# HGRN scores of a hybrid decoder trunk: two heads at a time with the levels sent one by one, against four heads at a time with the levels copied and sent as one block

## The chip, the cores and the metric

The kernel runs on one core of a Trainium2 chip, in one launch. The core has five engines with an instruction queue each: TensorE (PE; matrix products, with the loads of its stationary operand shown as PEld), VectorE (DVE), ScalarE (ACT), GpSimd (POOL) and SyncE (SP), which here only issues transfers. The metric is the device time of one execution in microseconds. Before the change it was 1250.81 us, the median of 3 runs (1249.93 to 1252.86). A chance given below is for a time that is faster or slower by more than 0.2%.

## The reference, cut to what matters

The model is a trunk of four layers on 256 tokens of width 1024. Layers 0 and 3 mix tokens with HGRN2, layer 1 with an mLSTM, layer 2 with S5; each is followed by a SwiGLU block of 2816 hidden columns. Only HGRN2 is touched here:

```python
q, f, v, g = jnp.split(x @ w_in, 4, axis=-1)
log_f = jnp.logaddexp(jnp.log(lb), jnp.log1p(-lb) + jax.nn.log_sigmoid(f))
k = (1.0 - lb) * jax.nn.sigmoid(-f)
q = jax.nn.silu(q)
...
    b = jnp.cumsum(lfb, axis=2)
    decay = jnp.exp(jnp.where(mask[:, :, None], b[t] - b[s], -jnp.inf))
    att = jnp.einsum('bhtd,bhsd,bhtsd->bhts', qb, kb, decay)
    o = att @ v + (q * exp(b)) @ s_prev
...
o = _head_rmsnorm(o, norm_w) * jax.nn.silu(g)
return o @ w_out
```

There are 8 heads with 128 key channels each. The score of query token t and key token s is a sum over the channels of q[t] k[s] times the product of the forget gates of all tokens from s+1 to t. The lower bound lb is zero in layer 0 and is not in layer 3.

## The kernel before

All weights come from HBM in float32, in blocks of 128 x 2048 (1 MB). `stage_next` (L113) splits each block for the products: ScalarE casts a half of 1024 columns to its high part (`hi`, L150), VectorE takes the difference as its low part (`lo`, L151), and `mm3` (L178) does a product as three, high by high, low by high and high by low (L181 to L183). Four blocks of such halves can be held; a block is staged one block ahead of its use (`AHEAD`), and the transfers are issued by SyncE in the order of the list that `plan` (L1362) writes. A projection with the weights as the stationary operand (`ws_block`, L198; two heads per block, 48 products of 256 columns) gives gates and queries with channels on the partitions; `as_part` (L185) gives values and output gates with tokens on the partitions, in products of 512 columns. `pieces` (L510) cuts such a projection into four pieces of 12 products that can be placed between other work.

The HGRN stage (`hgrn`, L485) runs in this order: values of the first half of the heads, the gates of all four head pairs (`hgrn_gates`, L606; five steps on ScalarE and two on VectorE for a pair, and four more on ScalarE where there is a lower bound), a change of ScalarE's table set, the queries of two pairs, and then the scores. `hgrn_scores` (L626) is a generator for one pair of heads. The tokens of the two halves of the sequence lie in one tile; the second half is reversed, so that both halves share each operation. The scores within blocks of tokens are built in levels m = 1, 2, 4, ... 64. At level m the keys of one block of m tokens meet the queries of the next block. Before a level, keys and queries have been multiplied up with the gate products that reach to the border between the two blocks; after it, they are multiplied on (`mul(x, x, whose(e, m, y))`, L683) and the gate products are paired (L687). This is the walk.

What goes to TensorE in a pair: 16 narrow products for the diagonal (L650), 8 for each of m = 1 to 16 (L664), 8 for m = 32 and 8 for m = 64 (L673), all with a stationary operand of 32 columns, each into one quarter of the partitions; and 2 full products for the scores across the two halves (L696). For m below 32 ScalarE first copies the keys of the level into `kk` (L660), and VectorE writes the results into the 32 x 32 blocks of the tile `near` with `copy_predicated` under a mask (L667). At m = 32 VectorE copies `near` into the score tile (L676), and ScalarE copies the levels 32 and 64 there (L680). Each level ends with a `yield`.

`scores` (L575) advances the generators of two pairs in turn, one level each, and puts other work between the levels:

```python
scores((0, 1), ([], [lambda: query(2)], [], [lambda: query(3)], v1[0:1], v1[1:2], v1[2:3], v1[3:]))
scores((2, 3), ([lambda: late.append(heads_out(0))], g0[0:1], ...
```

`heads_out` (L534) multiplies the scores of four heads with the values (L544, L546), squares and sums for the norm of the heads; `turn` (L560) gates the result and transposes it (`head_turn`, L448, L452); `out_proj` (L427) is the output projection with the two layer norms.

The framework's planner orders each engine's instructions: it takes the ready instruction of the highest priority (the order in the program) by a cost model, and sets all semaphores. `order` (L140) and the table dependencies in `act` and `table` (L82 to L99) are edges that only fix an order in this plan. Tiles with the same tag share a set of buffers; the banks of PSUM come in tags "a" (4), "g" (2) and "t" (2).

Of the kernel before, what the change touches and what calls it, by code (L numbers as in the profile page):

```python
# [28 lines left out]
MASKED = (1, 2, 4, 8, 16)  # L29
BIG = 1e30  # L30
# [4 lines left out]
class Trunk:  # L35
# [449 lines left out]
    def hgrn(self, j, gb, lb=None):  # L485
# [3 lines left out]
        with tc.tile_pool(name=self.uid("hg"), bufs=1, reuse_waits="tile") as hp, \  # L489
                tc.tile_pool(name=self.uid("hw"), bufs=2, reuse_waits="tile") as wp:  # L490
            msk = hp.tile([P, len(MASKED) + 1, 64], F32, name=self.uid("msk"))
            atts = [hp.tile([P, 512], F32, name=self.uid("att")) for _ in range(3)]
            for t in atts:
                nc.gpsimd.memset(t, 0.0)
            ot = self.transposed(hp)
# [38 lines left out]
            def heads_out(n):  # L534

                ss = self.small.tile([P, 2, 4], F32, tag="ss", name=self.uid("ss"))
                po = [self.bank("a") for _ in range(2)]
                for h in range(2):
                    for e in range(4):
                        hd = 4 * n + e  # L540
                        att, cross = mem[hd // 2]
                        c = slice(hd * P, (hd + 1) * P)
                        o = po[h][:, e * P : (e + 1) * P]
                        nc.tensor.matmul(o, att[:, 2 * h + hd % 2, :], v[:, h, c], start=True, stop=h == 0)  # L544
                        if h:
                            nc.tensor.matmul(o, cross[:, hd % 2, :], v[:, 0, c], start=False, stop=True)  # L546
# [5 lines left out]
                def scaled():  # L552
                    for h in range(2):
                        on[n, h] = wp.tile([P, 512], F32, tag="q", name=self.uid("on"), bufs=4)
                        f4 = lambda x: x.rearrange("p (a b) -> p a b", a=4)
                        nc.vector.tensor_tensor(f4(on[n, h]), f4(po[h]), r[:, 4 * h : 4 * h + 4, None].broadcast_to([P, 4, P]), ALU.mult)
# [8 lines left out]
            mem, q, pre, on = {}, {}, {}, {}  # L565

            def query(pr):
                pq = pair_proj(4 + pr, "a")
                q[pr] = wp.tile([P, 512], F32, tag="q", name=self.uid("q"), bufs=4)
                self.act(q[pr], pq, AF.Silu)  # L570

            def gates(pr):
                pre[pr] = self.hgrn_gates(wp, pr, pair_proj(8 + pr), lb)

            def scores(prs, fill):  # L575

                runs = [self.hgrn_scores(wp, q[pr], *pre[pr], msk, atts[pr % 3]) for pr in prs]
                for todo in fill:
                    for pr, run in zip(prs, runs):
                        mem[pr] = next(run)  # L580
                    for f in todo:
                        f()
# [3 lines left out]
            self.table("natural_log_exp_and_others")  # L586
# [19 lines left out]
    def hgrn_gates(self, wp, pr, pf, lb):  # L606

        nc, act = self.nc, self.act
        k, f = (wp.tile([P, 512], F32, tag=t, name=self.uid(t), bufs=4) for t in "kf")
# [3 lines left out]
        act(l, l, AF.Ln, bias=1.0)  # L613
        nc.vector.scalar_tensor_tensor(f, pf, 0.0, l, ALU.min, ALU.subtract)
# [3 lines left out]
        if lb is not None:  # L618
            for i in range(2):
                hd = slice(2 * pr + i, 2 * pr + i + 1)  # L620
                x, y = (t.rearrange("p (h a t) -> p a h t", h=2, a=2)[:, i] for t in (f, k))
                act(x, x, AF.Identity, scale=lb[:, 1, hd], bias=lb[:, 0, hd])
                act(y, y, AF.Copy, scale=lb[:, 1, hd])
        return k, f

    def hgrn_scores(self, wp, q, k, f, msk, att):  # L626

# [11 lines left out]
        keys = lambda t, m: view(t, 0, (256 + m, 2), (2 * m, P // m), (1, m))  # L639
        queries = lambda t, m: view(t, m, (256 - m, 2), (2 * m, P // m), (1, m))  # L640
        whose = lambda e, m, s: view(e, s, (2 * P // m + 1 - 2 * s, 2), (2, P // m), (0, m))
        four = lambda x: x.rearrange("p (a t) -> p a t", a=4)
        heads = lambda x: x.rearrange("p (a t) -> p a t", a=2)
        rows = lambda c: slice(32 * c, 32 * c + 32)
        near = wp.tile([P, P], F32, tag="near", name=self.uid("near"))
        k4, q4, a4 = four(k), four(q), four(att)
        pd = self.bank("a")[:, 0:P]
        for i in range(4):
            for c in range(4):
                nc.tensor.matmul(pd[rows(c), rows(i)], k4[:, i, rows(c)], q4[:, i, rows(c)], start=True, stop=True)  # L650
        nc.vector.tensor_tensor(four(near), four(pd), msk[:, len(MASKED), None, 0:32].broadcast_to([P, 4, 32]), ALU.mult)
        mul(q, q, f)
        e, ends = f, wp.tile([P, 256], F32, tag="ends", name=self.uid("ends"))
        spare = 0
        for m in (1, 2, 4, 8, 16, 32, 64):
            n = P // (2 * m)
            pl = self.bank("a")
            if m < 32:
                kk = wp.tile([P, 2 * P], F32, tag="kk", name=self.uid("kk"))
                nc.scalar.copy(view(kk, 0, (m, 2), (2 * m, 2 * n), (1, m)), keys(k, m))  # L660
                pl = pl[:, 0:64]
                for i in range(2):
                    for c in range(4):
# [854 lines left out]
```

## Time and profile before

| What | Value |
| --- | --- |
| median of 3 runs | 1250.81 us (1249.93 to 1252.86) |
| the profiled execution's own time | 1250.21 us |
| span of the profile | 1248.4 us |
| TensorE, VectorE, ScalarE busy | 1228.9, 957.0, 694.1 us |
| granted TensorE clock | 0.998 |
| in 13 to 130 us (layer 0's HGRN): TensorE, VectorE, ScalarE | 116.84, 92.48, 73.43 us |
| in 920 to 1046 us (layer 3's HGRN): the same | 125.13, 97.21, 79.25 us |

The span runs from the first to the last instruction. In rows of the order of time the columns are start, length, engine, line, operation, output and inputs, shape, count; equal instructions that follow each other are merged into one row. A product of two float32 tiles shows as two records, a product of the split parts as one. In rows of groups the numbers behind the bar are the busy time, the mean length of one in ns, and the idle time before them with what ended it. The end of a matmul is modelled, so the distance between starts says more than the length.

### The profile page before, as it was taken

To read this page: it belongs to the slowest core of one execution; us is meant where nothing else is said; L and a number is where in the kernel's file an instruction comes from. 1 tells how busy PE (TensorE), PEld (TensorE's weight loads), DVE (VectorE), ACT (ScalarE), POOL (GpSimd) and SP (SyncE) were. 2 spreads that over 40 slices of the span, in tenths; PEclk is the share of its full clock that TensorE was granted. 3 is DMA by queue.
4 is the path that set the end of the run, shared out by engine and by line. 5 is a ranking of instruction groups with operands and counts; after the bars stand their busy time and mean duration, and the time that the engine had idled before them with its cause. 6 is when DMAs were issued, how large, how long until landed. Compare 5 with 4: busy or idle time off the path is not lost.

```text
span 1248.4 us, 21395 instructions
## 1 busy us (share of the span) xinstructions
PE 1228.9 (98%) x8464; PEld 1030.2 (83%) x8464; DVE 957.0 (77%) x1717; ACT 694.1 (56%) x1126; POOL 34.7 (3%) x60
## 2 busy tenths in 40 slices
PE   9999999999999999999998999999999999999997
PEld 7978888888798888888886788888889878888886
DVE  6887879797787799887599787666486887766664
ACT  6755575565467555555444355555359653555551
POOL 0000100000100100000000000000000000000000
PEclk9999999999999999999999999999999999999999
DMA  8833376666273278767656456555446432755530
GB/s 313 303 136 136 142 276 221 214 223 236 97 301 135 102 277 300 240 249 249 219 203 222 169 191 248 189 182 202 169 180 216 155 133 104 268 186 185 195 143 34
DMA packets 50244, 247.91 MB, mean 199 GB/s; under 512 B 6336, under 2 KB 15952, under 8 KB 23776
## 3 DMA queue, kind: packets, MB, share of 16 engines
q1 hardware_dynamic: 50016, 246.46, 54.9%
q8 instruction: 66, 1.08, 0.3%
q14 instruction: 34, 0.28, 0.1%
q0 software_dynamic: 128, 0.09, 0.0%
HBM read 233.94 MB, written 12.58 MB: 197 GB/s over the span
## 4 chain that ended last, share of the span: by engine, by line
PE 89%; DVE 5%; DMA 2%; ACT 2%; issue 1%; SPq 0%; DVEq 0%; POOL 0%; ACTq 0%
PE g L211 18%; PE g L181 10%; PE g L183 10%; PE g L182 10%; PE g L214 9%; PE a L182 8%; PE a L181 8%; PE a L183 8%; DVE lo L151 1%; PE a L370 1%; PE t L272 1%; DMA bc<-in_s_bc 1%; PE a L664 1%; DMA first<-in_first 1%; PE a L544 1%; DVE s5rot L1218 1%
## 5 line engine op out<-in xcount | busy, mean ns | idle before, releaser
L151 DVE TENSOR_TENSOR lo<-w,hi 128x1024 fp32r<-128x1024 f32 x388 | 470.9, 1222 | 117.2 <-ACT hi L150 109.8
L150 ACT CAST hi<-w 128x1024 fp32r<-128x1024 f32 x388 | 405.1, 1051 | 186.7 <-PE a L182 95.6
L211 PE MATMUL g<-xx,hi 128*128 128x512 f32 x1024 | 356.4, 397 | 0.4 <-DVE sum L352 0.3
L214 PE MATMUL g<-xx,lo 128*128 128x256 f32 x1024 | 264.9, 279 | 0.0
L211 PEld LDWEIGHTS g<-xx,hi 128*128 128x128 f32 x1024 | 186.0, 188 | 37.1 <-DVE sum L352 1.1
L214 PEld LDWEIGHTS g<-xx,lo 128*128 128x128 f32 x1024 | 193.2, 189 | 10.9
L181 PE MATMUL g<-hi,xx 128*128 128x512 f32 (+1 forms) x416 | 166.3, 401 | 3.0 <-ACT xx L291 2.0
L183 PE MATMUL g<-lo,xx 128*128 128x512 f32 (+1 forms) x416 | 164.0, 396 | 0.1
L182 PE MATMUL g<-hi,xx 128*128 128x512 f32 (+1 forms) x416 | 163.2, 393 | 0.0
L182 PE MATMUL a<-hi,hl 128*128 128x512 f32 x328 | 129.5, 395 | 0.0
L183 PE MATMUL a<-lo,hh 128*128 128x512 f32 x328 | 129.4, 395 | 0.0
L181 PE MATMUL a<-hi,hh 128*128 128x512 f32 x328 | 129.0, 394 | 0.0
L351 ACT COPY sum<-g 128x256 f32<-128x256 f32 x128 | 47.7, 372 | 142.3 <-PE g L211 142.1
L352 DVE TENSOR_TENSOR sum<-g,sum 128x256 f32<-128x256 f32 x128 | 54.1, 423 | 61.8 <-ACT sum L351 61.3
L181 PEld LDWEIGHTS g<-hi,xx 128*128 128x128 f32 x416 | 78.2, 188 | 20.0 <-ACT xx L291 3.5
L183 PEld LDWEIGHTS g<-lo,xx 128*128 128x128 f32 x416 | 78.1, 188 | 17.5 <-DVE lo L151 1.9
L182 PEld LDWEIGHTS g<-hi,xx 128*128 128x128 f32 x416 | 78.3, 188 | 14.6
L182 PEld LDWEIGHTS a<-hi,hl 128*128 128x128 f32 x328 | 61.6, 188 | 14.6 <-DVE hl L341 0.5
L183 PEld LDWEIGHTS a<-lo,hh 128*128 128x128 f32 x328 | 61.7, 188 | 13.5
L181 PEld LDWEIGHTS a<-hi,hh 128*128 128x128 f32 x328 | 61.6, 188 | 13.1 <-ACT hh L340 0.5
L181 PE MATMUL g<-xx,hi 128*128 128x256 f32 x192 | 54.5, 284 | 0.0
L183 PE MATMUL g<-xx,hi 128*128 128x256 f32 x192 | 54.5, 284 | 0.0
(307 smaller groups left out, 1733.7 us busy)
## 6 DMA issues: line engine op xcount, KB each, us to landing
w<-in_w_gu SPq DMA_DIRECT2D x88, 1024.0 KB
w<-in_w_dn SPq DMA_DIRECT2D x44, 1024.0 KB
w<-in_w_hg SPq DMA_DIRECT2D x30, 1024.0 KB
w<-in_w_ml SPq DMA_DIRECT2D x12, 1024.0 KB
gb<-in_ln SPq DMA_DIRECT2D x8, 1024.0 KB
w<-in_w_ho SPq DMA_DIRECT2D x8, 1024.0 KB
w<-in_w_so SPq DMA_DIRECT2D x8, 1024.0 KB
w<-in_w_mo SPq DMA_DIRECT2D x4, 1024.0 KB
```

The costliest lines, as they stand in the source:

```text
L150: self.nc.scalar.copy(hi, x)
L151: i = self.nc.vector.tensor_tensor(lo, x, hi.bitcast(F32), ALU.subtract).ins
L181: mm(ps, lh, rh, start=start, stop=False)
L182: mm(ps, ll, rh, start=False, stop=False)
L183: mm(ps, lh, rl, start=False, stop=stop)
L211: whole = lambda: mm(ps, hi[:, c], self.xx[:, k].rearrange("p i t -> p (i t)"), start=k == 0, stop=k == KD - 1)
L214: mm(ps[:, S:], lo[:, c], self.xh[:, k], start=False, stop=False)
L272: nc.tensor.transpose(pt[:, (k % 4) * P : (k % 4 + 1) * P], z[:, k * P : (k + 1) * P], self.ident)
L351: nc.scalar.copy(t, ps[:, S:])
L352: nc.vector.tensor_tensor(t, ps[:, 0:S], t, ALU.add)
L370: nc.tensor.matmul(down[h][n], hidden(h, j, b)[x], dn[j][b][y][:, f], start=False, stop=(x, y, b) == steps[-1])
L544: nc.tensor.matmul(o, att[:, 2 * h + hd % 2, :], v[:, h, c], start=True, stop=h == 0)
```

## The change

`hgrn_scores` now works on four heads (a quad): its tiles of keys, queries and gates have 1024 columns instead of 512, and the multiplications of the walk cover four heads each. The levels m = 1 to 32 no longer go to TensorE as the walk gets to them. For each, ScalarE copies the level's keys and its queries into buffers (`saved`), and the walk goes on. When all six have been multiplied through, one block of instructions sends the level 64 and then the saved levels to TensorE (`tiny`, with an order edge behind the walk's last multiplication), into two PSUM banks. Five masked copies into `near` on VectorE follow, then copies into the score tile on ScalarE, the one of `near` among them. The diagonal products also have an edge that keeps them together.

`hgrn` asks for gates and queries of two pairs, begins the walk of the first quad, and puts the gates and queries of the other two pairs and two pieces of values behind it in the program; the score block of the first quad comes after these. The second quad follows in the same way, with pieces of values and output gates. ScalarE's table set is now changed four times in a stage instead of twice. There is one score tile in place of three; `near`, `ends` and `cross` have one buffer; the tiles of the transposed output are allocated at the end, in the buffers of the saved levels. The masks become wider, and the list of weights follows the new order.

```diff
+NEAR = MASKED + (32,)
...
             def query(pr):
                 pq = pair_proj(4 + pr, "a")
-                q[pr] = wp.tile([P, 512], F32, tag="q", name=self.uid("q"), bufs=4)
-                self.act(q[pr], pq, AF.Silu)
+                self.act(part(pr // 2, "q", pr), pq.rearrange("p (h x) -> p h x", h=2), AF.Silu)
...
-            for pr in range(4):
-                gates(pr)
+            gates(0)
+            gates(1)
             nc.sync.dma_start(msk, self.a["c_lvl"])
             nc.sync.dma_start(nw, self.a["hg_nw"][j])
-            self.table("silu_and_others")
+            self.table(silu)
             query(0)
             query(1)
             v1 = pieces(v, AF.Copy, 0, 1)
             g0, g1 = (pieces(g, AF.Silu, 12, n) for n in range(2))
-            scores((0, 1), ([], [lambda: query(2)], [], [lambda: query(3)], v1[0:1], v1[1:2], v1[2:3], v1[3:]))
-            late = []
-            scores((2, 3), ([lambda: late.append(heads_out(0))], g0[0:1], g0[1:2] + [lambda: late.pop()()], g0[2:3], g0[3:], g1[0:1], g1[1:2], g1[2:3]))
+            first = scores(0)
+            walk(0, first, len(NEAR))
+            self.table(exp)
+            gates(2)
+            gates(3)
+            self.table(silu)
+            query(2)
+            query(3)
+            v1[0]()
+            v1[1]()
+            walk(0, first)
+            second = scores(1)
+            walk(1, second)
+            v1[2]()
+            walk(0, first)
+            walk(1, second, len(NEAR) - 1)
+            v1[3]()
+            g0[0]()
+            g0[1]()
+            late = heads_out(0)
+            g0[2]()
+            late()
+            for f in g0[3:] + g1[:3]:
+                f()
+            walk(1, second)
+            g1[3]()
+            walk(1, second)
             gb = gb()
-            g1[3]()
+            ot = tuple(hp.tile([P, KD, S], F32R, tag="o", name=self.uid(n), bufs=2) for n in ("oh", "ol"))
...
-        for m in (1, 2, 4, 8, 16, 32, 64):
-            n = P // (2 * m)
-            pl = self.bank("a")
-            if m < 32:
-                kk = wp.tile([P, 2 * P], F32, tag="kk", name=self.uid("kk"))
-                nc.scalar.copy(view(kk, 0, (m, 2), (2 * m, 2 * n), (1, m)), keys(k, m))
...
+        for i in (2, 3, 6, 7, 0, 1, 4, 5):
             for c in range(4):
-                nc.tensor.matmul(pd[rows(c), rows(i)], k4[:, i, rows(c)], q4[:, i, rows(c)], start=True, stop=True)
+                mm = nc.tensor.matmul(pd[rows(c), rows(i)], k8[:, i, rows(c)], q8[:, i, rows(c)], start=True, stop=True).ins
+                self.order(mm, lead)
+                lead = lead or mm
...
+        for g, m in enumerate(NEAR):
+            n = 512 // m
+            kc, qc = saved[2 * g : 2 * g + 2]
+            nc.scalar.copy(view(kc, 0, (m, 2), (2 * m, 256 // m), (1, m)), keys(k, m))
+            nc.scalar.copy(view(qc, 0, (256, 2), (m, 256 // m), (1, m)), queries(q, m))
+            for x, y in ((keys(k, m), 1), (queries(q, m), 0)):
+                last = mul(x, x, whose(e, m, y)).ins
+            new = ends[:, 0:n]
+            if m > 1:
+                new, spare = f[:, spare : spare + n], spare + n
+            mul(new, e[:, 0::2], e[:, 1::2])
+            e = new
             yield
+        pl = [self.bank("a") for _ in range(2)]
+
+        def tiny(o, x, y):
+            self.order(nc.tensor.matmul(o, x, y, start=True, stop=True).ins, last)
...
+        level = lambda g: pl[g // 4][:, g % 4 * P : (g % 4 + 1) * P]
+        for g, m in enumerate(NEAR):
+            kc, qc = saved[2 * g : 2 * g + 2]
+            for a in range(4):
+                for c in range(4):
...
+                    tiny(o, kc[:, a * P + 32 * c :][:, 0:32], y)
+        for g, m in enumerate(MASKED):
+            three = lambda x: x.rearrange("p (h b m) -> p h b m", h=2, m=m)
+            nc.vector.copy_predicated(view(near, m, (P - m, 2), (2 * m, 64 // m), (1, m)), three(i32(msk[:, g * P : (g + 1) * P])), three(level(g)))
+        for c in range(4):
+            nc.scalar.copy(a8[rows(c), :, rows(c)], eight(near[rows(c)]))
...
-            p += [("w_hg", j, s) for s in (0, 1, 8, 9, 10, 11, 4, 5, 6, 7, 2, 3, 12, 13, 14, 15)] + [("w_ho", j, s) for s in range(4)]
+            p += [("w_hg", j, s) for s in (0, 1, 8, 9, 4, 5, 10, 11, 6, 7, 2, 3, 12, 13, 14, 15)] + [("w_ho", j, s) for s in range(4)]
```

More of the change, by code (lines that the diff above doesn't have):

```diff
@@ L646, in hgrn_scores @@
-        k4, q4, a4 = four(k), four(q), four(att)
-        pd = self.bank("a")[:, 0:P]
-        for i in range(4):
+        keys = lambda t, m: view(t, 0, (512 + m, 2), (2 * m, 256 // m), (1, m))
+        queries = lambda t, m: view(t, m, (512 - m, 2), (2 * m, 256 // m), (1, m))
+        whose = lambda e, m, s: view(e, s, (512 // m + 1 - 2 * s, 2), (2, 256 // m), (0, m))
+        eight = lambda x: x.rearrange("p (a t) -> p a t", a=8)
+        heads = lambda x: x.rearrange("p (a t) -> p a t", a=4)
@@ new lines, in hgrn_scores @@
+        rows = lambda c: slice(32 * c, 32 * c + 32)
+        near = wp.tile([P, 256], F32, tag="near", name=self.uid("near"), bufs=1)
+        levels = [hp.tile([P, 2048], F32, tag="o", name=self.uid("lev"), bufs=2) for _ in range(2)]
+        levels.append(wp.tile([P, 2048], F32, tag="lev", name=self.uid("lev"), bufs=1))
+        saved = [t[:, i * 512 : (i + 1) * 512] for t in levels for i in range(4)]
+        k8, q8, a8 = eight(k), eight(q), eight(att)
+        pd = self.bank("a")[:, 0:256]
@@ new lines, in hgrn_scores @@
+        for x, h in ((k8, 0), (q8, 4)):
+            x = x[:, h : h + 4, 0:64]
+            mul(x, x, e.rearrange("p (a s) -> p a s", s=2)[:, h : h + 4, 1:].broadcast_to([P, 4, 64]))
+        yield
+        pc = self.bank("a")
+        for a in range(4):
+            nc.tensor.matmul(pc[:, a * P : (a + 1) * P], k8[:, a], q8[:, 4 + a], start=True, stop=True)
+        cross = wp.tile([P, 4, P], F32, tag="cross", name=self.uid("cross"), bufs=1)
+        nc.scalar.copy(cross, heads(pc))
+        yield a8, cross
```

121 lines of the change are left out of this document (48 added, 73 removed).

## The prediction, made before the result was known

> **What bounds the kernel now.** I read the page first, then the order of time on TensorE inside the two HGRN stages (layer 0, about 13 to 130 us; layer 3, about 920 to 1046 us), because the diff touches nothing else.
>
> ```profile
> PE 1228.9 (98%) x8464; PEld 1030.2 (83%) x8464; DVE 957.0 (77%) x1717; ACT 694.1 (56%) x1126; POOL 34.7 (3%) x60
> PE 89%; DVE 5%; DMA 2%; ACT 2%; issue 1%; SPq 0%; DVEq 0%; POOL 0%; ACTq 0%
> ```
>
> TensorE is busy 98% of the span and is 89% of the chain that ended last. So time can only go by giving TensorE less to do, or lost time that it shows as "busy". That second kind exists. Here is TensorE in layer 0, with scores (L650, L664) between projections (L181 to L183); the first column is the start.
>
> ```profile
> 52.13 0.28 PE L182 MATMUL a<-xx,lo 128*128 128x256 f32 x1
> 52.25 0.28 PE L183 MATMUL a<-xx,hi 128*128 128x256 f32 x1
> 52.46 0.46 PE L650 MATMUL a<-q,k 128*32 128x32 f32 x32
> ...
> 53.88 0.39 PE L182 MATMUL g<-hi,xx 128*128 128x512 f32 x1
> 54.20 0.33 PE L664 MATMUL a<-q,kk 128*32 128x32 f32 x16
> 54.34 0.48 PE L650 MATMUL a<-q,k 128*32 128x32 f32 x32
> 54.76 0.50 PE L183 MATMUL g<-lo,xx 128*128 128x512 f32 x1
> 55.09 0.40 PE L181 MATMUL g<-hi,xx 128*128 128x512 f32 x1
> ...
> 98.63 0.40 PE L181 MATMUL g<-hi,xx 128*128 128x512 f32 x1
> 98.86 0.39 PE L182 MATMUL g<-hi,xx 128*128 128x512 f32 x1
> 99.18 0.33 PE L664 MATMUL a<-q,kk 128*32 128x32 f32 x16
> 99.44 0.50 PE L183 MATMUL g<-lo,xx 128*128 128x512 f32 x1
> 99.78 0.40 PE L181 MATMUL g<-hi,xx 128*128 128x512 f32 x1
> ```
>
> Look at starts, not durations. Two 512-column matmuls in a row start 0.23 us apart (98.63, 98.86), two of 256 columns 0.12 us. From 98.86 to 99.78 there are two large matmuls (0.46 us) and one run of 16 narrow records: 0.92 us, so the run costs 0.46 us. From 53.88 to 55.09 there are two large ones and 48 narrow records: 1.21 us, so 0.75 us. The difference, 0.29 us for 32 records, is 0.009 us a record; what is left, 0.46 − 16 × 0.009, is a fixed **0.315 us for each time that TensorE turns from 128-wide to 32-wide weights and back**. It lies in three places: a late start of the run, a late start of the first large matmul, and 0.33 us instead of 0.23 to the next one (54.76 to 55.09). No row calls it idle.
>
> ```profile
> L664 PE MATMUL a<-q,kk x640: 191/196/219, 54.2 to 1012.6; 128*32 128x32 f32 x160
> L650 PE MATMUL a<-q,k x256: 192/196/218, 52.5 to 999.3; 128*32 128x32 f32 x128
> L673 PE MATMUL a<-q,k x256: 195/217/244, 74.0 to 1018.4; 128*32 128x32 f32 x64, 128*32 128x64 f32 x64
> ...
> 1017.93 0.65 PE L673 MATMUL a<-q,k 128*32 128x64 f32 x32
> ```
>
> These 1152 records (576 per layer, two for each of 288 narrow matmuls) sit in 23 separate runs per layer, counted in the order of time from the row at 52.46 to 104.59 us, and again from 968.72 to the row at 1017.93. So 46 × 0.315 = 14.5 us of the kernel are turns.
>
> **The change part by part.**
>
> *Fewer runs.* The new program has 32 + 16 + 96 = 144 narrow matmuls for four heads, 288 per layer: as many records as now, with the same widths (32 columns; 64 for the level m = 64). Only their grouping changes. The diagonal blocks (formerly L650) are held together by an order edge, and all levels come in one block after the last multiplication of the walk, on inputs that were saved before. That is two runs for four heads, 4 per layer in place of 23. 19 × 2 × 0.315 = **−12.0 us**. The diagonal run of the second four heads may touch the first level run: −0.3 us per layer at best; I take 0. Whether a run of 224 records keeps its pace is seen in the S5 stage:
>
> ```profile
> 646.61 1.99 PE L1202 MATMUL g<-s5u,bm 128*32 128x64 f32 x128
> 648.53 0.39 PE L182 MATMUL a<-hi,xx 128*128 128x256 f32 x1
> ```
>
> 128 records of 64 columns in 1.92 us are 0.015 us each, twice the columns at under twice the price of mine; the pace holds.
>
> *Work on VectorE and ScalarE.* Groups of layer 3 (mean ns after the comma):
>
> ```profile
> L636 DVE TENSOR_TENSOR q<-q,f 128x256 f32<-128x256 f32 x20 | 8.4, 421 | 0.0
> L636 DVE TENSOR_TENSOR q<-q,f 128x512 f32<-128x512 f32 x4 | 2.7, 684 | 0.0
> L667 DVE COPY_PREDICATED near<-msk,a 128x64 f32<-128x64 int32 x20 | 5.1, 256 | 2.2 <-PE a L664 1.9
> L676 DVE COPY att<-near 32x128 f32<-32x128 f32 x16 | 3.5, 216 | 0.2
> L150 ACT CAST hi<-w 128x1024 fp32r<-128x1024 f32 x30 | 31.1, 1045 | 17.4 <-PE g L182 10.8 <-PE a L183 4.5 <-DMA w<-in_w_hg 2.1
> L660 ACT COPY kk<-k 128x256 f32<-128x256 f32 x20 | 7.7, 414 | 3.5 <-PE a L664 1.9 <-DVE k L636 1.4
> L94 ACT ACTIVATE t<-t 128x512 f32<-128x512 f32 x8 | 5.0, 629 | 0.0
> L94 ACT ACTIVATE f<-f,odds 128x256 f32<-128x256 f32 x8 | 4.7, 590 | 0.0
> ```
>
> VectorE: two multiplications of 256 columns (0.84 us) become one of 512 (0.68): 40 of those of keys and queries become 20, −3.1 us per layer. Twenty masked copies of 64 become ten of 128, put between 0.256 and 0.42 us (a 256-column operation), say 0.31: −2.0 us. The 16 copies L676 go to ScalarE: −3.5 us. VectorE gets 8.6 us lighter per layer. ScalarE loses 20 copies of 0.41 us (8.3) and gains 24 of 512 columns at 0.63 (15.1), 8 diagonal copies (estimate 0.3 each, between 0.216 and 0.41: 2.4) and two table loads: about +12 us per layer. None of this is on TensorE's path by itself; the question is whether ScalarE still delivers the casts that the projections wait for.
>
> ```profile
> 931.60:954.60 23.00, 23.00 (x192) 22.92 (x191) 14.18 (x16) 19.90 (x33) 0.00 (x0) 1.00 0.78 280
> 954.60:968.70 14.10, 14.10 (x106) 13.22 (x104) 7.97 (x9) 13.54 (x23) 0.00 (x0) 1.00 0.49 176
> 968.70:996.90 28.20, 28.06 (x432) 23.09 (x432) 25.73 (x71) 17.69 (x37) 0.00 (x0) 1.00 0.42 152
> 52.50:79.90 27.40, 27.29 (x429) 22.49 (x429) 23.73 (x70) 15.82 (x33) 0.00 (x0) 1.00 0.47 171
> ```
>
> Columns: window, length, busy PE, PEld, DVE, ACT, POOL, clock, DMA share, GB/s. Today the gates fill ScalarE (13.54 of 14.10) and the walks leave it slack (17.69 of 28.20), while VectorE is nearly full in the walks. After the change the first walk lies beside the gates and queries of the second four heads and two pieces of values: 4 × 48 × 0.12 + 2 × 12 × 0.23 = 28.6 us of TensorE. ScalarE's bill there: 12 copies 7.5, ten gate steps 6.3, two loads 2.6, two queries 1.2, ten casts 10.5: 28.1 us in layer 0, which just fits. Layer 3 adds 8 steps for the lower bound, at most 4.7: 32.8 us against 28.6. So between 0 (the last gate steps, queries and loads may slip past the score run, which doesn't need them) and 4.2 us of stall; I take the middle, **+2.0 us**. In the second walk no gates are left, and that stretch fits.
>
> The table loads are priced by these rows:
>
> ```profile
> 966.27 0.50 ACT L94 ACTIVATE k<-k,odds 128x256 f32<-128x256 f32 x1
> 966.77 1.28 ACT L87 ACT_TABLE_LOAD   x1
> 968.07 1.08 ACT L94 ACTIVATE q<-a 128x512 f32<-128x512 f32 x2
> ```
>
> The load takes 1.28 us, and the operations before and behind it touch it: 1.30 us in all. [...]
>
> *The tail of the stage.* Now the last levels come out long before the last heads need them. Afterwards the second level run is followed only by one gate piece (12 × 0.23 = 2.8), the cross products and the turning of the first heads, and then the output of the last four heads.
>
> ```profile
> 114.40 1.04 PE L452 MATMUL t<-ident,on 128*128 128x128 f32 x8
> 115.27 1.28 PE L544 MATMUL a<-v,att 128*128 128x128 f32 x10
> ```
>
> The turning lasts 0.87 us, the cross products about as much: 4.5 us of cover. Against it: five masked copies (1.6), four diagonal copies (1.2) and a wait behind a cast or a low half (1.0 to 1.2): 4 us. Without the cover it would cost those 4 us twice. Between 0 and 1.5 us per layer; I take 0.5, **+1.0 us**.
>
> *At nothing.* The single near tile makes VectorE wait, once per layer, until ScalarE has copied the old one out (four copies, 1.2 us); behind it in the queue stand the walk and the low halves, and the 8.6 us that VectorE saves cover that; uncovered, at most 1.2 us. The mask transfer grows by 672/384 on SP's queue and is issued past other weights than before; the weights swap places at equal size, and DMA is busy 0.42 to 0.47 in the walks. Uncovered it would cost a transfer of a third of a weight block. One output tile for both halves and the late allocation of the turned heads wait for reads that lie before them on TensorE anyway.
>
> Sum: −12.0 + 2.0 + 1.0 = −9.0 us. The profiled execution took 1250.21 us (span 1248.4 and 1.8 around it): 1241.2. The median shown is 0.6 above it, inside its own spread of 2.9, so I forecast **1241**.
>
> **The rivals.**
>
> *ScalarE becomes the bound.* All that does not fit shows, the loads and walk copies not slipping anywhere: 4.2 in layer 3 and, with ScalarE kept waiting for VectorE between the levels of the walk as it is for a tenth of the time now (3.5 us idle before L660), 3.5 more in each layer. +11.2 instead of +2.0: 1250, no change. For it: 13.54 of 14.10. Against: the planner sees these costs and can put pieces of values ahead. 0.12.
>
> *The runs are not runs.* The order edges hold only the planner's order; where inputs are late it may slip projections between. Each of the 4 runs of a layer cut three times: 2 × 12 × 0.315 = 7.6 given back: 1248.6. Against: all level inputs are saved before the last multiplication. 0.08.
>
> *The walk becomes a chain in series* (the other side). A level now is copy, multiply, next copy: 0.63 + 0.68 us, and behind a cast and a low half (1.05 + 1.22) 3.6 us; six levels and 4.4 us at the front (the diagonal mask 0.4, the decay on the queries 1.2, the old masked and diagonal copies 2.8) are 26, against 28 of cover (nine pieces of 12 × 0.23, the first heads' output and cross products). If each level waits behind two casts and two low halves it is 5.85 us, 39.5 in all; the second walk is then 11.5 us late, of which one gate piece hides 2.8, and the mask copies (4 us) follow uncovered: 12.7 us per layer lost against 6.0 won, 1264. It decides from 4.7 us per level, where loss and gain are equal. Against: today the first four heads take the window of 27.4 us, with VectorE busy 23.73 of it, and VectorE gets less to do. 0.10.
>
> **How the numbers follow.** Forecast 0.70, with its own range 1236 (no stall, merged runs) to 1246 (4.2 and 1.5 per layer). ScalarE 0.12, cut runs 0.08, chain 0.10. The range 1236 to 1250 leaves out the chain and little else. A measurement of this kernel can tell about 0.2%, 2.5 us. Faster (below 1248.3): the forecast and about a third of the two middle rivals and some of the chain's mild forms: 0.80. Same: 0.09. Slower: 0.11.
>
> **What would show it.** In the order of time on TensorE: one unbroken run of about 224 narrow records twice per layer, each some 2.3 us to the next large matmul; wrong if they are cut. Between runs, large matmuls 0.23 us apart with no wait above 0.3 us; a wait for ScalarE's casts in layer 3 just before the first level run is the ScalarE rival, a wait for near or att before the last heads is the tail. Layer 0 should shrink by 5 to 6 us and layer 3 by 3 to 5. The forecast is wrong if layer 0 does not shrink.

## The result and the profile after

The changed kernel takes **1261.25 us** (median of four runs, 1260.01 to 1264.81) against 1251.23 before (four runs, one more than above, 1249.93 to 1252.86): a ratio of 1.0084 with a 95% interval of 1.0071 to 1.0098. It is 10 us slower, where I had forecast 1241 and had put 1250 at the upper end.

The page of the changed kernel, first the engines' busy times, then the chain that ended last, then the queue that brings instructions (packets, MB, share):

```profile
PE 1223.9 (97%) x8464; PEld 1034.3 (82%) x8464; DVE 944.7 (75%) x1577; ACT 713.8 (57%) x1126; POOL 33.3 (3%) x56
...
q8 instruction: 66, 1.08, 0.3%
...
PE 91%; ACT 4%; issue 2%; DVE 2%; DMA 1%; POOL 0%; SPq 0%; DVEq 0%; ACTq 0%
```

VectorE is 12 us lighter and ScalarE 20 us heavier in both layers together, where I had worked out 17 and 24. TensorE is busy 5 us less, yet the span is 10 us longer. "issue" has gone from 1% to 2% of the chain: time in which TensorE waited for nothing that the profile knows. Before looking for it, a ledger. The same matmul, counted from the start, closes the stage in both kernels (numbers 100 to 1300 for layer 0, 6206 to 7500 for layer 3), so the elapsed time between them compares like with like; "turns" is what the first narrow and the first and second wide matmul of each change start later than their pitch, and the rest is sorted in the same way.

```
us, layer 0 + layer 3        before             after
elapsed                      109.76 + 126.06    114.53 + 132.35   (+11.1)
turns                          7.48 +   7.57      1.32 +   1.58   (-12.1)
unreleased gaps over 1 us      0    +   0         6.99 +   9.31   (+16.3)
wide matmuls late              0.50 +   0.93      2.83 +   3.64   ( +5.0)
waits for data over 0.4 us     0    +   0         1.17 +   0      ( +1.2)
narrow matmuls late           -0.34 +  -0.24      0.11 +   0.03   ( +0.7)
```

The turns were saved, to a tenth of a microsecond. The narrow records stand in three runs per layer, of 64, 288 and 224 records: the diagonal of the second quad (L673) runs on from the first quad's level run (L696; its first 32 records, 64 columns wide, are the level m = 64). So 46 turns have become 6, not 8. What came in their place stands in the order of time on TensorE (start, duration; in brackets the idle time ahead of a group and its releaser), for the four long runs, the 288 and the 224 of each layer:

```profile
70.57 1.73 PE L696 MATMUL a<-lev 128*32 128x32 f32 x171
74.47 0.35 PE L696 MATMUL a<-lev 128*32 128x32 f32 x19 [2.17 <-issue]
...
105.18 0.65 PE L696 MATMUL a<-q,k 128*32 128x64 f32 x32
105.65 1.31 PE L696 MATMUL a<-lev 128*32 128x32 f32 x126
111.41 1.17 PE L696 MATMUL a<-lev 128*32 128x32 f32 x66 [4.44 <-issue]
112.51 0.80 PE L182 MATMUL g<-hi,xx 128*128 128x512 f32 x1
113.10 0.63 PE L183 MATMUL g<-hi,xx 128*128 128x512 f32 x1
113.53 0.63 PE L184 MATMUL g<-lo,xx 128*128 128x512 f32 x1
...
989.42 0.56 PE L673 MATMUL a<-q,k 128*32 128x32 f32 x40
994.84 0.54 PE L673 MATMUL a<-q,k 128*32 128x32 f32 x22 [4.86 <-issue]
...
1025.65 1.86 PE L696 MATMUL a<-lev 128*32 128x32 f32 x189
1031.59 0.25 PE L696 MATMUL a<-lev 128*32 128x32 f32 x3 [4.08 <-issue]
```

Every long run stops once, 2.4 to 5.1 us from start to start. In three of them the records left behind the stop read the same saved levels as those ahead of it (in the one at 989.42 it is the diagonal), and the last stop comes three records from the end. After 111.41 the wide matmuls start 0.43 us apart (113.10, 113.53) instead of 0.23. The view of busy time by stretch (length, then busy PE, PEld, DVE, ACT and POOL with instructions, granted clock, DMA share, GB/s) shows both:

```profile
106.50:109.00 2.50, 0.46 (x54) 0.35 (x40) 1.26 (x2) 0.00 (x0) 0.00 (x0) 1.00 0.89 367
109.20:110.20 1.00, 0.00 (x0) 0.00 (x0) 0.00 (x0) 0.00 (x0) 0.00 (x0) 1.00 0.00 0
110.20:111.40 1.20, 0.00 (x0) 0.00 (x0) 0.00 (x0) 0.00 (x0) 0.00 (x0) 0.53 0.00 0
112.50:117.20 4.70, 4.70 (x13) 3.74 (x12) 1.07 (x4) 3.31 (x10) 0.00 (x0) 0.51 0.02 3
117.30:121.00 3.70, 3.70 (x34) 3.66 (x33) 1.03 (x2) 3.41 (x7) 0.00 (x0) 1.00 0.00 0
```

From 109.2 to 111.4 no engine of the core does anything, and the data queues are still. TensorE isn't waiting for an operand that someone is making. And the clock falls to half (0.51 in the stretch up to 117.2). The waits of the changed kernel sum it up (sum, times, longest):

```profile
PE a L696 <- issue: 10.7, 3, 4.4
...
PE a L673 <- issue: 4.9, 1, 4.9
PE t L1283 <- issue: 4.7, 3, 2.6
```

The last of these rows is the S5 stage, which the change doesn't touch. The kernel before has it too, under another line number. Its waits come to:

```profile
PE t L1248 <- issue: 3.5, 3, 1.7
```

And two of those three places in its order of time, with VectorE's row ahead of the first:

```profile
657.14 1.18 DVE L1227 TENSOR_TENSOR s5hs<-s5rot,s5rot 128x1024 f32<-128x1024 f32 x1
658.43 1.16 PE L1248 MATMUL t<-ch,s5hs 64*64 64x64 f32 x64 [1.67 <-issue]
...
671.07 0.69 PE L1248 MATMUL t<-ch,s5hs 64*64 64x64 f32 x30
672.77 0.74 PE L1248 MATMUL t<-ch,s5hs 64*64 64x64 f32 x34 [1.01 <-issue]
```

The row of waits was there to be read before I predicted. Its longest wait, 1.67 us, is of another kind, though: TensorE's queue has an instruction there that waits for a semaphore until 658.38, just after VectorE has made `s5hs`, which the matmul reads. The profile merely doesn't name the releaser. The other two, and all the stops inside the long runs, have no such instruction: nothing in TensorE's program waits there.

**Theory F (fetch).** 66 packets of 16,384 bytes bring 1.08 MB. TensorE's 8464 matmuls, 8464 weight loads and some 80 other instructions make 17,011 in the trace, 258 to a packet. I take 256 for a block, which is 128 narrow records with their weight loads; this is an estimate from those counts, and the stops below bear it out. I counted TensorE's instructions from the start of the trace up to each stop, and set beside it when the count passed the same place one block earlier, and the next packet of that queue:

```
kernel, stop     count mod 256   one block earlier   packet             resumes   gap
after     72.10       192              70.98          71.83 -  73.06      74.47   2.37
after    106.77       193             105.61         109.14 - 110.10     111.41   4.64
after    989.78       192             988.64         992.62 - 993.56     994.84   5.05
after   1027.31       193            1026.22        1029.24 - 1030.20   1031.59   4.27
after    675.72       192 (S5)        673.30         676.19 - 677.08     678.54   2.82
before   671.54       192 (S5)        669.18         670.03 - 671.32     672.77   1.23
before   683.38       192 (S5)        680.77         681.68 - 683.06     684.40   1.02
```

All stand at the same place by this count, 192 or 193, which I call a border, and all end 1.3 to 1.5 us behind the end of a packet. So the theory: at a border TensorE goes on only when the packet that belongs to it has come, and in these seven stops it went on 3.5 to 6.2 us after the border before. All ten traces of this case bear it out: if the packets are set in order beside the places that stand at 193 mod 256 (one packet to a place, the first beside the second place), TensorE never passes a place less than 1.1 us after its packet has ended (651 places), and each unreleased idle time over 0.7 us that has no semaphore instruction ends 1.1 to 1.6 us after the packet of its place. In the first four rows the 128 records from one border to the next took 1.09 to 1.16 us. So by the theory a run that holds two borders runs dry. Before, wide matmuls always lay between: in the two HGRN stages the borders are 5.8 us or more apart.

Rivals: **D**, the stop is a wait for late copies that the profile fails to name (against it already: no semaphore instruction stands there); **P**, the narrow tiles themselves stop after so many records; **C**, the half clock is the loss and the gaps lie beside something else.

### The profile page after: what moved, and what is told of

It reads as the page before. It is cut to its first block, busy times and chain, and to the rows that moved or that the text cites. A ratio compares the mean times of both kernels' runs of the same rounds, so it can differ in the third digit from the quotient of the medians.

```text
span 1258.2 us, 21154 instructions
## 1 busy us (share of the span) xinstructions
PE 1223.9 (97%) x8464; PEld 1034.3 (82%) x8464; DVE 944.7 (75%) x1577; ACT 713.8 (57%) x1126; POOL 33.3 (3%) x56
## 3 DMA queue, kind: packets, MB, share of 16 engines
q8 instruction: 66, 1.08, 0.3%
## 4 chain that ended last, share of the span: by engine, by line
PE 91%; ACT 4%; issue 2%; DVE 2%; DMA 1%; POOL 0%; SPq 0%; DVEq 0%; ACTq 0%
PE g L212 19%; PE g L182 10%; PE g L215 9%; PE g L184 9%; PE g L183 9%; PE a L183 9%; PE a L184 9%; PE a L182 9%; PE a L371 1%; PE t L273 1%; PE a L696 1%; ACT hi L151 1%; PE g L1237 1%; DMA first<-in_first 1%; DVE lo L152 0%
## 5 line engine op out<-in xcount | busy, mean ns | idle before, releaser
L215 PE MATMUL g<-xx,lo 128*128 128x256 f32 x1024 | 264.6, 279 | 0.0
L184 PE MATMUL g<-xx,hi 128*128 128x256 f32 x192 | 54.5, 284 | 0.0
L183 PE MATMUL g<-xx,lo 128*128 128x256 f32 x192 | 54.4, 283 | 0.0
```

The costliest lines, as they stand in the source:

```text
L183: mm(ps, ll, rh, start=False, stop=False)
L184: mm(ps, lh, rl, start=False, stop=stop)
L215: mm(ps[:, S:], lo[:, c], self.xh[:, k], start=False, stop=False)
```

## The experiments

The quoted expectations say "pair" for what the text above calls a quad. Those of the kernels in portions also say "diagonal" for the 32 wide records that come with the level m = 64.

**The program moved by 24 records.** Line numbers shift by two in this kernel.

```diff
         self.nc.tensor.matmul(ps, z[:, 0:P], z, start=True, stop=True)
+        for _ in range(24):
+            self.nc.tensor.matmul(ps[:, 0:32], z[:, 0:P], z[:, 0:32], start=True, stop=True)
```

> 24 small matmuls (32 columns) are added to the warm-up at the start, so that every later instruction of TensorE stands 48 places further on in its program; nothing else differs from the changed kernel. Theory F (TensorE's program comes in blocks of 256 instructions, which is 128 narrow records, and a long narrow run reaches the end of the blocks at hand before the next has come): the four unreleased gaps stay, but come 24 records earlier in their runs: in layer 0 after 179 records of the level run (203 in the changed kernel: 32 and 171) and after 134 of the second (158: 32 and 126), in layer 3 after 242 (266) and after 197 (221: 32 and 189). Counted in TensorE's instructions from the start, each is again at 192 or 193 mod 256. 2 to 5 us each, time 1259 to 1264. Rival P (the narrow tiles themselves stop after so many records): gaps after the same counts as before, 203, 158, 266, 221. Rival D (a copy or product of the saved levels arrives late): gaps before the operands that they stood before in the changed kernel, so again 203, 158, 266, 221.

Measured: 1255.67 us in one run, beside 1250.34 of the kernel before; 1259 to 1264 was expected. What counts here is the place of the stops. The order of time in layer 0:

```profile
71.13 1.51 PE L698 MATMUL a<-lev 128*32 128x32 f32 x147
74.72 0.47 PE L698 MATMUL a<-lev 128*32 128x32 f32 x34 [2.08 <-issue]
...
105.93 0.65 PE L698 MATMUL a<-q,k 128*32 128x64 f32 x32
106.40 1.89 PE L698 MATMUL a<-lev 128*32 128x32 f32 x192
108.22 0.50 PE L184 MATMUL g<-hi,xx 128*128 128x512 f32 x1
```

The first stop comes after 32 + 147 = 179 records in place of 203, and those of layer 3 after 242 and 197: 24 earlier each, at 192 or 193 of a block again. P and D, which have them after the old counts, are out. The second run of layer 0 has no stop at all, which I had not foreseen, and which makes the kernel faster than expected: 224 records in one go, 2.3 us. There the border falls six records into the run, and the packet was under way at 104.50, ahead of the run's start at 105.93, while the wide matmuls still ran. Why the packet was that early my count doesn't say; the theory tells where a run can stop, not that it must.

**The long runs later.** The first run moves behind all value pieces, the second behind all gate pieces.

```diff
-            v1[0]()
-            v1[1]()
+            for f in v1:
+                f()
             walk(0, first)
...
-            for f in g0[3:] + g1[:3]:
+            for f in g0[3:] + g1:
                 f()
-            walk(1, second)
-            g1[3]()
-            walk(1, second)
+            walk(1, second, 2)
```

> The level runs are placed later: the first pair's behind all four value groups of the second pair's stage, the second pair's behind all of its gate groups; so the copies that they read are 5.5 us (first) and 2.8 us (second) older when TensorE gets there. Nothing else differs from the changed kernel. Theory F: a gap of 2 to 5 us remains in each level run, with its place moved by the matmuls that now stand ahead of it (in layer 0 after about 179 and 146 records, in layer 3 after about 242 and 210), at 192 or 193 mod 256 of TensorE's instructions; time 1257 to 1264. Rival D: with the copies older than any wait seen, no gap remains and the time is 1240 to 1245. Rival P: gaps after the counts of the changed kernel (203, 158, 266, 221), time as the changed kernel.

Measured: 1256.43 us in one run, just under the range. Two of its places in the order of time:

```profile
112.01 0.91 PE L692 MATMUL a<-lev 128*32 128x32 f32 x78 [2.28 <-issue]
...
113.84 1.04 PE L453 MATMUL t<-ident,on 128*128 128x128 f32 x8
117.72 2.50 PE L543 MATMUL a<-v,att 128*128 128x128 f32 x10 [2.85 <-ACT att L720]
...
1026.68 1.76 PE L692 MATMUL a<-lev 128*32 128x32 f32 x177
1030.45 0.33 PE L692 MATMUL a<-lev 128*32 128x32 f32 x15 [2.01 <-issue]
```

All four stops are there, where F has them (78 and 15 records from the end of 224, so after 146 and 209), although the operands are microseconds older. That settles D. The stops are shorter, 2.2 to 2.5 us, and this has a reason that the records show: here the packets start 1.0 to 1.5 us after the count passes one block earlier. In the three stops over 4 us of the changed kernel it takes 3.0 to 4.0 us, and in two of them the packet starts at the very time when the last packet of a 1 MB weight transfer ends (109.14 and 1029.24), with the DMA engines busy 0.83 and 0.76 of the time from the count to there. That looks as if the block had queued behind the transfer, but busy DMA engines alone don't make the delay: from 70.5 to 71.9 us, ahead of the first stop of the changed kernel, they were busy 0.93, and the packet started 0.85 us after the count. What makes the longer delays stays open. The gain is spent elsewhere: with no wide work behind the run, TensorE now waits 2.85 us for ScalarE's copies, and after that wait too it is at half speed (the ten matmuls of L543 take 2.50 us here, 1.28 in the kernel before).

**Two portions.** 128 records, 24 wide matmuls, 96 records.

```diff
+PORTIONS = ((None, 0, 1, 2), (3, 4, 5))
...
-        for g, m in enumerate(NEAR):
+        for i, portion in enumerate(PORTIONS):
+            if i:
+                yield
+            for g in portion:
+                far() if g is None else close(g)
```

`far` is the loop of the level m = 64, `close(g)` the body of the loop over the levels; each `yield` lets the stage put projection pieces in.

> The level run of 224 records is sent in two portions, 128 records (second quad's diagonal with levels 1, 2, 4) and 96 (levels 8, 16, 32), with two pieces of 128-wide work (24 large matmuls) between; the operands, the copies and the number of matmuls are those of the changed kernel. 6 narrow runs to a layer in place of 4 (46 turns in both layers and the last before, 12 now). Theory F: a portion of at most 128 records holds at most one border of blocks, and the sequencer has the large matmuls to catch up in: no unreleased gap over 1 us in layers 0 and 3, but for at most one of 0 to 2.3 us at the second pair's diagonal run of layer 3, which still joins levels; the half clock behind the gaps is gone too. Time: before less (46 - 12) x 0.315 = 10.7 us, so about 1240, 1236 to 1245. Rival P (stops after a number of records in one run above some 130): also no gaps, the same time. Rival D: gaps stay where late data is read; 1255 to 1262. Rival C (the half clock alone is the loss, whatever causes it): gaps of the same sum, without half clock, 1255.

**Four portions**, 64, 64, 64 and 32 records with 12 wide matmuls between.

```diff
+PORTIONS = ((None, 0), (1, 2), (3, 4), (5,))
```

> The level run is sent in four portions of 64, 64, 64 and 32 records, one piece of 128-wide work (12 large matmuls) between each; operands, copies and the number of matmuls are those of the changed kernel. Some 10 narrow runs to a layer. Theory F: gaps of 1 to 2 us in all in layers 0 and 3, since no 160 records stand without 128-wide work; more turns than with two portions: before less (46 - 20) x 0.315 = 8.2 us, so about 1243, 1239 to 1247. Theory of my prediction, turns alone: the same 1243; it would be slower than the two portions by 8 x 0.315 = 2.5 us. Rival D: gaps stay, 1256 or more.

Measured: 1253.45 us for two portions, ratio 1.0026 (1.0016 to 1.0036), and 1250.28 for four, 0.9995 (0.9986 to 1.0005). In both, no unreleased gap over 1 us is left in layers 0 and 3, and the half clock behind the gaps is gone; with two portions it comes once in these layers, at 1000.4 us, behind a wait of 2.16 us for ScalarE's move of the values. C is out: by the ledger the gaps cost 16.3 us by themselves, and the half clock came behind idle time, of whatever cause. But the gain expected did not come. In the order of time of the four portions stand waits with a name:

```profile
96.97 0.65 PE L695 MATMUL a<-q,k 128*32 128x64 f32 x32 [1.65 <-DVE q L654]
...
122.37 1.23 PE L454 MATMUL t<-ident,on 128*128 128x128 f32 x8 [1.28 <-DVE on L563]
```

The second quad's first portion, which begins with the level m = 64, now stands ahead of its last operand, and the last portion so late that the chain behind it (masked copies, output, scaling) has less cover. Both come again in layer 3; with 0.5 us at another place that is 7.0 us in the two layers, and it is 9.4 us with two portions. My expectation had costed the portions as if the place among the pieces were free.

**Three portions, placed by those rows.** First quad 96, 64, 64; second quad 96 and 128, or 64, 64 and 96, with the level m = 64 last, since its queries are ready last, and more wide work behind. The cut shows the second quad of the kernel with 64, 64 and 96.

```diff
+PORTIONS = (((None, 0, 1), (2, 3), (4, 5)), ((0, 1), (2, 3), (4, 5, None)))
...
+            walk(1, second)
+            g0[3]()
+            walk(1, second)
+            g1[0]()
+            walk(1, second)
+            g1[1]()
+            g1[2]()
             walk(1, second)
             g1[3]()
...
```

(The other one has `((0, 1, 2), (3, 4, 5, None))` for the second quad and no portion ahead of `g0[3]`.)

> The narrow run of each pair of heads is sent in portions with 12 or more large products between, and placed so that nothing that the two earlier portioned kernels waited for is late: the first pair's 224 records as 96, 64, 64 with one value piece between, the second pair's as 96 (levels 1, 2, 4) and 128 (levels 8, 16, 32, then the diagonal blocks, whose queries come last), the latter two gate pieces ahead of the near products and three ahead of the final transposes. The matmuls, copies and operands are those of the changed kernel. 7 narrow runs to a layer. Theory F (a border of 256 instructions costs nothing when at least some 5 us lie between two borders): no unreleased gap over 1 us in layers 0 and 3 but for 0 to 1.6 us at the 128 records, if a bulk transfer is on its way then; time: before less (46 - 14) x 0.315 = 10.1 us, plus 0 to 3 us of waits for data, so 1240 to 1244. If the turns are worth less than I put them at, or the larger ScalarE and VectorE work has a price of its own, it stays at 1247 to 1251, as the four portions did.

> As the kernel with 96, 64, 64 and 96, 128 records, but the second pair's run as 64, 64, 96, the first of them one piece earlier. 8 narrow runs to a layer. Theory F: no unreleased gap over 1 us in layers 0 and 3; two turns more than the other, 0.6 us; time 1240 to 1245. If the first portion stands ahead of its operands (the levels 1 and 2 of the second pair), a wait of 0 to 2 us on VectorE or ScalarE shows there, and 1244 to 1248.

Measured: 1247.05 us, ratio 0.9969 (0.9958 to 0.9981), and 1247.44, ratio 0.9969 (0.9959 to 0.9979). Both beat the kernel before, by less than expected. What is left in the second kernel, in TensorE's order of time:

```profile
82.58 0.50 PE L183 MATMUL g<-hi,xx 128*128 128x512 f32 x1 [1.22 <-ACT v L523]
```

And on ScalarE ahead of it:

```profile
78.32 1.69 ACT L736 COPY att<-near 32x256 f32<-32x256 f32 x4 [1.55 <-DVE near L734]
80.03 1.88 ACT L741 COPY att<-a 32x128 f32<-32x128 f32 x6
81.93 1.09 ACT L523 ACTIVATE v<-g 128x512 f32<-128x512 f32 x2
```

The ten copies into `att` stand in ScalarE's queue ahead of the move of the values, and TensorE waits for the banks. The changed kernel has a wait for the same move (1.00 us, at 83.24); there the ten copies end at 78.8 us, and copies of the second quad's levels, a cast and another copy stand between.

**The first quad's portions one piece earlier** than in the kernel with 64, 64 and 96, so that those ten copies are done by then; and the same with 64 records more at the start, half a block.

```diff
+            walk(0, first)
             v1[0]()
             walk(0, first)
             v1[1]()
             walk(0, first)
             v1[2]()
-            walk(0, first)
             v1[3]()
```

> As the kernel with 96, 64, 64 and 64, 64, 96 records, but the first pair's three portions each stand one value piece earlier, so that ScalarE has the copies out of the banks behind it when the last value piece is to be moved. Theory F with the wait that the kernel with 64, 64, 96 records still had (large products behind the near products, waiting 1.22 us in each layer for ScalarE's copy of the values): that wait goes, no other comes in its place: no unreleased gap over 1 us in layers 0 and 3, 2.4 us less than 1247.4, so 1244 to 1246, 0.5% under the kernel before. If ScalarE is short as such, the wait only moves, and the time stays at 1247.

> The kernel with the portions one value piece earlier, with 64 small matmuls added to the warm-up, which moves every later border of 256 instructions by half a block. Theory F: in portions it is of no account where in them a border falls, since two borders are never closer than about 4 us: no unreleased gap over 1 us in layers 0 and 3, and the time of the unshifted one within 2 us (0 to 2 us may go into the longer warm-up itself). If the portions only helped because the borders happened to fall well, gaps of 2 to 5 us come back.

Measured: **1244.34 us**, ratio 0.9960 (0.9947 to 0.9972), and 1246.29, ratio 0.9967 (0.9955 to 0.9979) with the borders moved. The wait for the values is gone, no unreleased gap over 1 us is in layers 0 and 3 of either, and the clock stays up (around the first quad's portions of layer 0, then the second's):

```profile
62.00:80.00 18.00, 18.00 (x363) 14.80 (x362) 8.66 (x14) 11.08 (x21) 0.00 (x0) 1.00 0.53 199
88.00:112.00 24.00, 24.00 (x337) 20.02 (x336) 17.63 (x31) 16.07 (x29) 2.26 (x2) 1.00 0.27 93
```

By the ledger the faster one saves 9.6 us of turns and pays 3.6 us of waits for data, all of them behind the last portion, where the heads' outputs are scaled, turned and projected. Part of these is new: with the values on time TensorE reaches the projection earlier and waits 0.56 and 0.61 us for ScalarE's `oh`. So the two layers became 1.0 us shorter (the ledger below), where I had expected 2.4. It is the change as it was meant, at 0.4% under the kernel before. With the borders half a block on, some lie only 2.4 us apart by my count (2.15 once in the unmoved kernel) and still nothing stops, so "4 us apart" in that expectation was not the condition. In both places the planner left a single wide matmul between two portions of 64 records, but many come ahead of them, and the packet starts 4.1 and 4.2 us ahead of the count, as with the 24 records, where it was 1.5 us ahead.

The S5 stage, which no version touches in its code, has one to three stops at borders in most versions, 1.0 to 3.2 us each from start to start, that differ from version to version, since its program moves too. The totals therefore differ by a few microseconds that have nothing to do with the HGRN layers, and the ledger counts only these (elapsed us between the same matmuls):

```
                     before    after     late    2 port.  4 port.  96/128  64/64/96  earlier
layer 0              109.76   114.53   113.83   109.89   109.41   108.03   107.57   106.91
layer 3              126.06   132.35   128.05   127.97   125.68   124.51   123.67   123.38
turns, both           15.05     2.90     2.04     4.65     6.06     4.39     5.26     5.43
waits for data, both   0        1.2      5.6      9.4      7.0      6.9      4.8      3.6
```

## Why the prediction was wrong

*Fewer runs, −12.0 us: right.* The ledger gives 12.1; 15.05 us for 46 turns is 0.327 us each, for my 0.315. The close agreement is partly luck: the second quad's diagonal joined the first level run, which I had taken at nothing, so 40 turns went and not 38, but the six that stayed cost 0.48 us each.

*"The pace holds": the step that failed.* I costed a run of 224 records by the pace of 128 records in the S5 stage. 128 records are just one block of TensorE's program, so that row could not show what a second border costs. The second border cost 16.3 us of gaps and about 5 us of half clock behind three of them, 21 in all against the 12 saved. With the gaps out of the way the rest of the sum is nearly enough: −12.1 + 1.2 + 0.7 is −10.2, where I had −9.0.

The row that spoke against it was among the waits of the kernel before: `PE t L1248 <- issue`, two of whose three waits are stops inside a run of small matmuls. I had read issue as 1% of the chain and asked no further. Where wide matmuls lay between the borders, in the HGRN stages of the kernel before, none shows a stop; inside the narrow runs one cost up to 5.05 us.

*ScalarE's shortage in layer 3's first walk, +2.0 us: not there.* No wait over 0.4 us but the two unreleased gaps stands in layer 3. The table loads cost their own time and no more, as I took it: in both stages ScalarE's next operation starts 1.29 to 1.30 us after each load of 1.28. One of them in the changed kernel:

```profile
983.17 0.51 ACT L95 ACTIVATE k<-k,odds 128x256 f32<-128x256 f32 x1
983.70 1.28 ACT L88 ACT_TABLE_LOAD   x1
985.00 0.60 ACT L95 ACTIVATE q<-a 128x512 f32<-128x512 f32 x1
```

*The tail, +1.0 us: too small, and hidden at first.* In the changed kernel the stops in the second runs gave ScalarE and VectorE the time they needed: in the kernel moved by 24 records, whose second run of layer 0 doesn't stop, TensorE waits there 0.59, 0.60 and 1.17 us for `att`, `cross` and `on`. With the stops gone and the portions well placed, 3.6 us of it show in the best version, 1.8 per layer, just over the 1.5 that I had as the upper end.

*At nothing:* the mask transfer and the single near tile show no wait. Giving the copies into `att` to ScalarE was not free: 1.38 us by the ledger in each layer with 96/128 or 64/64/96, as the values' move stood right behind them.

*The rivals.* The walk in series and the ScalarE bound did not come: in layer 0 the last saved level is copied at 55.2 us and its run starts at 70.1, in the second quad 88.7 and 105.2. "The runs are not runs" was nearest in what is seen, but its mechanism, wide work slipped between, is the cure here. None of my cases had a wait that belongs to the instruction stream itself, and the range, built from them, ended 11 us short.

## What to carry to other kernels

Count instructions as well as time. Eleven of the twelve long runs of the changed kernel, the moved one and the later one stopped: TensorE got through 256 instructions, 128 records with their weight loads, in 1.1 to 1.2 us, and went on 3.3 to 6.2 us after the place one block earlier. The profile shows such a stop only as "issue". Ask of an "issue" whether a semaphore instruction stands ahead of it; if one does, it is a wait for data after all. So join short matmuls to save turns, but keep slow ones between the groups, then look whose data the new places have made late. And a pace read from a run of one length is a price for that length only.

## What the runs showed of the hardware

In the eleven stops of layers 0 and 3 of the changed kernel, the moved one and the later one, the time from one block earlier by my count to the next matmul was 3.3 to 3.7 us in seven, and 5.4 to 6.2 us in four. Three of these four stand in the table above, with a packet that started 3.0 to 4.0 us behind the count.

In these runs the clock was halved after each of the four gaps over 4.2 us (4.27, 4.29, 4.64 and 5.05), for 2.9 to 5.7 us from where TensorE went on, and after the wait of 2.85 us for data (0.51 from 117.7 to 120.4 in the later kernel). After gaps of 2.2 to 2.5 us it was halved in some places (2.27, 2.44 and 2.50) and not in others (2.15, 2.21, 2.37 and 2.48); these are the later kernel's stretches right behind its gaps of 2.50 and 2.21 us:

```profile
998.40:1001.00 2.60, 2.58 (x55) 2.51 (x54) 1.67 (x3) 2.41 (x9) 0.00 (x0) 0.50 0.71 296
1030.45:1033.00 2.55, 2.29 (x31) 2.01 (x31) 0.30 (x1) 1.68 (x5) 0.00 (x0) 1.00 0.89 369
```

In the changed kernel, its last 5 us aside, half clock began at 110.27, 663.23, 994.32 and 1031.87 us and lasted 6.83, 3.41, 3.41 and 3.41 us; the last three of these began 162, 259 and 270 times 3.413 us after the first. In the 3.41 us ahead of them TensorE was busy 0.10, 1.59, 0.00 and 0.28 us, so in three of the four it had not been idle throughout. Why one gap of 2.2 to 2.5 us halved the clock and another did not is not shown.
